# Block sums of weights and gate halves: from GpSimd additions to copies and adding transfers in DRAM

## The chip, the cores and the metric

One Trainium2 chip, of which one core is used. A core has TensorE (PE in the profile), VectorE (DVE), ScalarE (ACT), GpSimd (POOL) and SyncE (SP), and 16 DMA engines which the queues of SP, ACT and POOL share. The metric is the device time of one execution of the kernel in microseconds, lower is better.

## The reference, cut to what matters

An encoder layer in float32, sequence 1024, model width 1024, feed-forward width 2816:

```python
mod = jax.nn.silu(c) @ w_ada + b_ada
sh1, sc1, gt1, sh2, sc2, gt2 = jnp.split(mod[:, None, :], N_MOD, axis=-1)
h = rmsnorm(x, norm1_g) * (1.0 + sc1) + sh1
u, v, q, k, va, gate_a, gate_b = jnp.split(h @ w_in, cuts, axis=-1)
a_out = gmlp_branch(u, v, gm_v_g, gm_w_s, gm_b_s) @ w_a
b_out = window_attention_branch(q, k, va, q_norm_g, k_norm_g, attn_sink) @ w_b
merged = jax.nn.sigmoid(gate_a) * a_out + jax.nn.sigmoid(gate_b) * b_out
x = x + gt1 * (merged @ w_o)
h2 = rmsnorm(x, norm2_g) * (1.0 + sc2) + sh2
f_gate, f_up = jnp.split(h2 @ w_ffn_in, 2, axis=-1)
x = x + gt2 * ((jax.nn.silu(f_gate) * f_up) @ w_ffn_out)
```

## The kernel before, in words

**Products.** Each float32 product is made of three products of rounded parts: high by high, high by low, low by high. `unit` turns a loaded tile `raw` (128 x 1024, 512 KB) into `wh`, cast by ScalarE, and `wl`, what is left, subtracted by VectorE (in the attention loops by GpSimd). There are three buffers each of `raw`, `wh` and `wl`. Activations are split in the same way.

**Blocks.** The products with w_u and w_v, with the gates' weights w_ga and w_gb, with w_o and the feed-forward weights are done as two by two blocks in seven block products rather than eight. That needs sums of the weights' four blocks and sums or differences of the activations' blocks. With blocks a11, a12 (of w_u or w_ga) and a21, a22 (of w_v or w_gb), the weights' sums are a21+a22, a11+a21+a22, a11+a21 and a12+a11+a21+a22. The sums of before are additions on GpSimd between tiles in SBUF.

**Stages**, with their place in the profiled execution:
- 0 to 65 us: projection of the first half of the sequence to q and k in eight steps (`half(0)`), beside the adaLN loads; from the first step on `x_square(k)` loads rows of the second half's x into an `hs` tile (two buffers), squares them on ScalarE and adds on GpSimd (L553).
- 65 to 110: the bridge: u and v products, norms of q and k (`kd`, `q_norm`), and `u_sums` (L870), which loads blocks of w_u and w_v, makes eight sums of 128 x 1024 on GpSimd and stores them to `usd` and `utd` (L244). `bridge_copy` (L745) stores the first products to `uvd`.
- 110 to 190: the attention loop of the first half, eight steps. Gate products (`gate_filler`, L809) fill TensorE's gaps; each evicts its bank through a `t` tile (four buffers) to `gd` in DRAM by ScalarE's queue (`astore`, L139). `x_mod` loads and modulates the second half's x and stores it to `x1sd`.
- 190 to 260: projection and bridge of the second half, with `block_sums` of activations on VectorE.
- 260 to 340: its attention loop. `gate_raw_sum` (L763) loads w_gb and half of w_ga and adds them on GpSimd.
- 340 to 425: the u and v stage: `load_uv` reads `uvd`, two GpSimd additions of 128 x 2048 (L1036 and L1037) merge them, then products, GELU, norm and mixing.
- 425 to 550: the loop over eight rows d of gates and branch projections. `gate_prep` (L1107) loads w_ga[d], w_gb[d] and gd[d] and makes five sums on GpSimd; `merge` stores the merged rows to `md` (L1180).
- 550 to 650: the products with w_o: `load_wo` (L1190) loads four 1 MB blocks, `wsum` (L1274) makes four sums on GpSimd; residual, gt1 scaling (`gated`) and sums of squares (`ssq`, L1293, additions on GpSimd by default).
- 650 to the end: the feed-forward part, which the change does not touch.

**What sets the order.** Each engine runs its instructions in program order; SP's loads and, within a half's loop, everything else are kept in the order in which the code is written (`in_order`). A DMA is issued by SP (`load`, L133), ScalarE (`astore`, L139) or GpSimd (`store`, L136), in line with that engine's other instructions. The work of a half's loop is a list of jobs: per step, one `run_jobs` and the fillers.

Every engine instruction goes through one wrapper, so the profile shows L75 for all of them; they are told apart by tile names.

## Time and profile before

| What | Value |
|---|---|
| Time, median of 3 runs | 1308.88 us (1307.22 to 1310.63) |
| The profiled execution's own time | 1312.13 us |
| Its span in the profile | 1310.3 us |
| Mean granted TensorE clock | 0.979 |
| TensorE busy | 1230.9 us (94%) |
| DMA moved | 261.17 MB, 199 GB/s over the span |

The profile is of one execution; durations read from it stand against its own 1312.13 us, and 3.25 us are taken off to compare with the median. "Busy" leaves out the issuing of DMAs. A table by stretch gives the busy time of each engine between two moments of the span; "released by" (<-) names what ended the idle time ahead of an instruction.

### The profile page before, as it was taken

Reading aid. Unit: us, or ns where it says so; the run is one execution under the profiler, and the core shown is the slowest. Engines: PE = TensorE matmul, PEld = TensorE weight load, DVE = VectorE, ACT = ScalarE, POOL = GpSimd, SP = SyncE. Lnnn points to the kernel's source line nnn. Section 1 sums busy time; section 2 is a strip of 40 time slices with the busy share of each in tenths; the row PEclk is TensorE's granted clock in tenths of the full one; section 3 lists DMA queues with packets and bytes.
Section 4 is the critical chain, followed back from the end, with each engine's and each line's share of the span. In section 5 each row is a group of like instructions: output and inputs, shape, how many; then the busy total and the mean of one; then the engine's idle time right before and its main releaser. Section 6 shows DMA issues by size and latency. Waiting matters only on the chain.

```text
span 1310.3 us, 15346 instructions
## 1 busy us (share of the span) xinstructions
PE 1230.9 (94%) x5522; PEld 1003.2 (77%) x5522; DVE 961.1 (73%) x1445; ACT 568.5 (43%) x928; POOL 281.6 (21%) x229
## 2 busy tenths in 40 slices
PE   6879998999969998988999999999999999999998
PEld 4757777887758777776788888888888887888887
DVE  8999868977587776789899766766665765555646
ACT  5447762677563121225555333333333333533342
POOL 1583320433362242263010001000001000010001
PEclk9998999999989999998999999999999999999999
DMA  9855468642734656641541344555437547986652
GB/s 366 304 220 216 159 249 286 231 140 98 296 138 177 256 226 234 247 193 65 183 155 49 113 161 175 202 195 199 146 143 243 191 162 262 322 306 205 193 173 97
DMA packets 82255, 261.17 MB, mean 199 GB/s; under 512 B 8706, under 2 KB 8706, under 8 KB 72835
## 3 DMA queue, kind: packets, MB, share of 16 engines
q1 hardware_dynamic: 61490, 175.25, 37.7%
q0 software_dynamic: 12624, 70.26, 14.7%
q10 hardware_dynamic: 8064, 14.68, 3.0%
q8 instruction: 43, 0.70, 0.2%
q14 instruction: 34, 0.27, 0.1%
HBM read 188.85 MB, written 71.30 MB: 199 GB/s over the span
## 4 chain that ended last, share of the span: by engine, by line
PE 64%; DVE 16%; DMA 10%; ACT 4%; issue 4%; POOL 1%; SPq 0%; ACTq 0%; DVEq 0%; POOLq 0%
PE at L75 40%; PE mm L75 24%; DVE mid L75 7%; DMA raw<-in_w_gb_dram 3%; DVE wl L75 3%; DVE j L75 2%; DMA raw<-in_w_q_dram 1%; ACT wh L75 1%; DMA mid<-in_xT_dram 1%; DVE kd L75 1%; POOL raw L75 1%; DMA mid<-in_w_ada_dram 1%; DMA md<-j 1%; DMA mid<-x0d 1%; ACT lb L75 1%
## 5 line engine op out<-in xcount | busy, mean ns | idle before, releaser
L75 PE MATMUL mm<-mid,wh 128*128 128x512 f32 x736 | 233.1, 398 | 1.7 <-DVE mid L75 1.7
L75 PE MATMUL at<-mid,wh 128*128 128x512 f32 (+1 forms) x728 | 228.7, 396 | 6.1 <-ACT mid L75 2.9
L75 DVE TENSOR_TENSOR wl<-raw,wh 128x1024 fp32r<-128x1024 f32 x116 | 153.8, 1326 | 81.6 <-ACT wh L75 81.3
L75 ACT CAST wh<-raw 128x1024 fp32r<-128x1024 f32 x126 | 131.8, 1048 | 116.4 <-PE at L75 38.1
L75 PEld LDWEIGHTS at<-mid,wh 128*128 128x128 f32 x728 | 138.6, 192 | 38.2 <-ACT mid L75 3.3
L75 PEld LDWEIGHTS mm<-mid,wh 128*128 128x128 f32 x736 | 138.3, 190 | 31.5 <-DVE mid L75 2.3
L75 PE MATMUL at<-mid,wl 128*128 128x512 f32 (+1 forms) x364 | 144.1, 396 | 8.9 <-DVE wl L75 8.9
L75 PE MATMUL mm<-mid,wl 128*128 128x512 f32 x368 | 145.6, 396 | 4.6 <-DVE wl L75 4.6
L75 PE MATMUL at<-j,wh 128*128 128x512 f32 (+1 forms) x464 | 143.6, 391 | 0.0
L75 PE MATMUL mm<-wh,mid 128*128 128x512 f32 x320 | 110.8, 414 | 11.6 <-DVE mid L75 6.5
L75 PEld LDWEIGHTS at<-j,wh 128*128 128x128 f32 x464 | 86.5, 188 | 20.2 <-DVE mid L75 0.2
L75 DVE TENSOR_TENSOR wl<-ws,wh 128x1024 fp32r<-128x1024 f32 (+1 forms) x55 | 62.0, 1127 | 44.2 <-ACT wh L75 44.2
L75 PE MATMUL at<-j,wl 128*128 128x512 f32 (+1 forms) x232 | 90.7, 391 | 0.0
L75 PEld LDWEIGHTS at<-mid,wl 128*128 128x128 f32 x364 | 69.8, 192 | 25.5 <-DVE wl L75 11.0
L75 PEld LDWEIGHTS mm<-mid,wl 128*128 128x128 f32 x368 | 70.1, 191 | 21.1 <-DVE wl L75 5.9
L75 PEld LDWEIGHTS mm<-wh,mid 128*128 128x128 f32 x320 | 63.0, 200 | 25.7 <-ACT mid L75 13.3
L75 ACT CAST wh<-ws 128x1024 fp32r<-128x1024 f32 (+1 forms) x55 | 53.5, 974 | 57.7 <-DVE ws L75 41.2
L75 PE MATMUL mm<-wl,mid 128*128 128x512 f32 x160 | 66.4, 415 | 0.4 <-DVE wl L75 0.4
L75 PE MATMUL mm<-j,wh 128*128 128x512 f32 x176 | 57.2, 406 | 4.9 <-DVE j L75 4.9
L75 DVE TENSOR_TENSOR ol<-raw,oh 128x1024 fp32r<-128x1024 f32 x30 | 36.7, 1224 | 32.4 <-ACT oh L75 30.6
L75 ACT ACTIVATE j<-j 128x512 f32<-128x512 f32 x32 | 19.9, 631 | 92.8 <-DVE j L75 92.8
L75 DVE TENSOR_TENSOR mid<-mid,mid 128x512 fp32r<-128x512 f32 (+3 forms) x43 | 50.6, 1209 | 8.8 <-DMA mid<-x1sd 5.1
(251 smaller groups left out, 2457.2 us busy)
## 6 DMA issues: line engine op xcount, KB each, us to landing
raw<-in_w_gate_dram SPq DMA_DIRECT2D x28, 512.0 KB, 4.7
j<-in_w_ada_dram SPq DMA_DIRECT2D x13, 1024.0 KB, 5.4
tA<-hid POOLq DMA_DIRECT2D x11, 1024.0 KB, 5.0
tB<-hid POOLq DMA_DIRECT2D x11, 1024.0 KB, 4.9
wo<-in_w_out_dram POOLq DMA_DIRECT2D x22, 512.0 KB, 6.3
wS<-wo POOLq DMA_DIRECT2D x11, 1024.0 KB, 5.5
raw<-wS SPq DMA_DIRECT2D x44, 256.0 KB, 3.4
raw<-tB SPq DMA_DIRECT2D x44, 256.0 KB, 4.4
```

Source lines behind the costliest of these rows:

```text
L75: ins = f(*args, **kw)
```

## The change

Twelve DRAM tensors hold the weights' block sums: `wus` for u and v, `wgs` for the gates, `wos` for w_o, 1 to 4 each. A sum is begun by `sum_copy`, a DMA from DRAM to DRAM of one block on ScalarE's queue, and finished by `sum_add`, a DMA from DRAM to DRAM on GpSimd's queue that adds its source to what lies there. There are 16 copies and 16 adds of 1 MB (the gates' in two halves): four copies in the last steps of the first half's projection, eight copies and eight adds, one a step, in its loop, four copies and eight adds in the second half's loop. Sums 2 and 4 add another sum: 2 adds sum 1, and 4 adds sum 2. The stages behind load finished sums.

The halves of the gates are merged in the same way: the first half's loop stores each first-half gate product to three columns of `gd` and each second one to the fourth, 32 stores instead of 16; the second half's loop adds its products to `gd` by 16 adding DMAs from SBUF. So with `uvd`: four stores in the first half, now on ScalarE's queue, and two adds of 1 MB in the second. In the w_o stage w_o's blocks and sums come through `raw` tiles, seven 1 MB blocks rather than four, two evictions scale by gt1 on ScalarE, and x is added to them by two adding DMAs. The squares' additions in `x_square` and `ssq` move to VectorE; `x_square` runs at steps 6 and 7 (0 and 1, then 2, 3, 4) and in the bridge (5, 6, 7).

```diff
@@ -243,3 +243,5 @@
     gd = rows_d(KT, "gd", w=2048)
-    usd, utd = rows_d(2, "usd", w=2048), rows_d(2, "utd", w=2048)
+    wus = [None] + [rows_d(2, f"wus{i}", w=UNIT) for i in range(1, 5)]
+    wgs = [None] + [rows_d(KT, f"wgs{i}") for i in range(1, 5)]
+    wos = [None] + [rows_d(1, f"wos{i}", w=2048) for i in range(1, 5)]
     md = [rows_d(KT, f"md{h}") for h in range(2)]
@@ -539,2 +541,27 @@
 
+    def acc_dma(dst, src):
+        ins = nc.gpsimd.dma_start(dst, src, accum_op=ALU.add, max_dma_last_dim=4096)
+        if in_order[0]:
+            tc.keep_in_program_order(ins)
+
+    SUMS = {}
+
+    def sum_begin(dst, src):
+        load(dst, src)
+
+    w_gah = [w_ga[:, :, i * Q : (i + 1) * Q] for i in range(2)]
+    w_gbh = [w_gb[:, :, i * Q : (i + 1) * Q] for i in range(2)]
+    SUMS["u"] = (wus, (w_u[0:2], w_u[2:4], w_v[0:2], w_v[2:4]))
+    SUMS["g0"] = ([x and x[0:4] for x in wgs], [x[0:4] for x in w_gah + w_gbh])
+    SUMS["g1"] = ([x and x[4:8] for x in wgs], [x[4:8] for x in w_gah + w_gbh])
+    SUMS["o"] = (wos, tuple(w_o[i : i + 1] for i in range(4)))
+
+    def sum_copy(n, i):
+        s, (a11, a12, a21, a22) = SUMS[n]
+        astore(s[i], {1: a21, 2: a11, 3: a21, 4: a12}[i])
+
+    def sum_add(n, i):
+        s, (a11, a12, a21, a22) = SUMS[n]
+        acc_dma(s[i], {1: a22, 2: s[1], 3: a11, 4: s[2]}[i])
+
     next_x = {}
@@ -552,3 +579,3 @@
             A.activation(q, xk, AF.Square)
-            G.tensor_tensor(ssn, ssn, q, op=ALU.add)
+            V.tensor_tensor(ssn, ssn, q, op=ALU.add)
 
@@ -686,3 +713,6 @@
                 store(x0d[k], x[:, :HALF])
-                x_square(k)
+                if k > 3:
+                    sum_copy(*(("u", 3), ("g0", 3), ("g1", 3), ("u", 1))[k - 4])
+                for i in ((), (0, 1), (2, 3, 4))[max(k - 5, 0)]:
+                    x_square(i)
             else:
@@ -725,3 +755,3 @@
         bsrc = [w_u[k] for k in range(4)] if hf == 0 else [
-            usd[0][:, :UNIT], usd[1][:, :UNIT], w_v[2], w_v[3]]
+            wus[3][0], wus[3][1], w_v[2], w_v[3]]
         bridge = [unit(bsrc[0], V)]
@@ -748,3 +778,7 @@
                 (V.tensor_copy if t % 2 else A.copy)(u[:, t, :], vps[t])
-            store(uvd[2 * hf + i], flat(u))
+            if hf:
+                acc_dma(uvd[2 + i], flat(u))
+            else:
+                for j in ((0, 2, 3), (1,))[i]:
+                    astore(uvd[j], flat(u))
 
@@ -764,6 +798,4 @@
             r = wpool.tile([P, UNIT], F32, tag="raw", name=nm("raw"))
-            load(r, w_gb[d])
-            x = stream("hs")
-            load(x, w_ga[d][:, :Q])
-            G.tensor_tensor(r[:, :Q], r[:, :Q], x, op=ALU.add)
+            load(r[:, :Q], wgs[3][d])
+            load(r[:, Q:], w_gb[d][:, Q:])
             return r
@@ -774,3 +806,3 @@
             srcs = [lambda d=d: gate_raw_sum(d) for d in range(KT)]
-            srcs += [utd[j][:, :UNIT] for j in range(2)]
+            srcs += [wus[2][j] for j in range(2)]
         units = []
@@ -820,4 +852,10 @@
                 A.copy(c, gbanks[d])
-                i = ((2, 0), (3, 1))[hf][ks[-1] // 4]
-                astore(gd[d][:, i * Q : (i + 1) * Q], c)
+                i = ks[-1] // 4
+                if hf:
+                    acc_dma(gd[d][:, (3 - 2 * i) * Q : (4 - 2 * i) * Q], c)
+                elif i:
+                    astore(gd[d][:, :Q], c)
+                else:
+                    for j in (1, 2, 3):
+                        astore(gd[d][:, j * Q : (j + 1) * Q], c)
             if ks[-1] == KT - 1:
@@ -869,14 +907,2 @@
 
-            def u_sums(j):
-                a, b = midt(F32, 2), midt(F32, 2)
-                for i in range(2):
-                    load(a[:, i, :], w_v[2 * i + j])
-                    load(b[:, i, :], w_u[2 * i + j])
-                return [lambda: G.tensor_tensor(a[:, 1], a[:, 0], a[:, 1], op=ALU.add),
-                        lambda: G.tensor_tensor(a[:, 0], a[:, 0], b[:, 0], op=ALU.add),
-                        lambda: (G.tensor_tensor(b[:, 0], b[:, 0], a[:, 1], op=ALU.add),
-                                 store(usd[j], flat(a))),
-                        lambda: (G.tensor_tensor(b[:, 1], b[:, 1], b[:, 0], op=ALU.add),
-                                 store(utd[j], flat(b)))]
-
 
@@ -893,3 +919,4 @@
         if hf == 0:
-            us = u_sums(0)
+            for i in (5, 6, 7):
+                x_square(i)
         bridge.append(unit(bsrc[2], V))
@@ -903,4 +930,2 @@
             col_rstd(next_x["ss"], NT, rcol[1])
-            for f in us:
-                f()
         bridge_product(2)
@@ -941,5 +966,2 @@
                 prepare(V)
-            if t == 0 and hf == 0:
-                for f in u_sums(1):
-                    f()
         bridge_copy(1)
@@ -949,2 +971,4 @@
             jobs.extend(lambda k=k: x_mod(k) for k in range(KT + 1))
+            wjobs = [("u", 3), ("g0", 3), ("g1", 3), ("u", 1), ("g0", 1), ("g1", 1), ("u", 2), ("g0", 2)]
+            cjobs = [("u", 2), ("g0", 1), ("g1", 1), ("g0", 2), ("g1", 2), ("u", 4), ("g0", 4), ("g1", 4)]
         else:
@@ -966,2 +990,4 @@
 
+            wjobs = [("g1", 2), ("u", 4), ("g0", 4), ("g1", 4), ("o", 3), ("o", 1), ("o", 2), ("o", 4)]
+            cjobs = [("o", 3), ("o", 1), ("o", 2), ("o", 4)]
             jobs.extend([lambda: None] * 3)
@@ -987,2 +1013,5 @@
                 values(base + i, koff, kv, pts, vts, i, oH, oL)
+            if cjobs:
+                sum_copy(*cjobs.pop(0))
+            sum_add(*wjobs.pop(0))
             fill(FB)
@@ -1016,3 +1045,3 @@
     t1f = jt(F32, 4)
-    uv_raw = [raw_unit(usd[0][:, UNIT:])]
+    uv_raw = [raw_unit(wus[1][0])]
     load(flat(t1f), t1d[0])
@@ -1026,6 +1055,6 @@
     load_uv(0)
-    uv_raw.append(raw_unit(usd[1][:, UNIT:]))
+    uv_raw.append(raw_unit(wus[1][1]))
     vgain_b = stream("hs")
     load(vgain_b, rowv[:GW].partition_broadcast(P))
-    uv_raw.append(raw_unit(utd[0][:, UNIT:]))
+    uv_raw.append(raw_unit(wus[4][0]))
     load_uv(2)
@@ -1035,4 +1064,2 @@
     lows(T1J, t1f)
-    G.tensor_tensor(flat(c2), flat(c2), flat(up1), op=ALU.add)
-    G.tensor_tensor(flat(c1), flat(c1), flat(up1), op=ALU.add)
 
@@ -1107,13 +1134,12 @@
     def gate_prep(d):
-        ga, gb = raw_unit(w_ga[d]), raw_unit(w_gb[d])
         g = gates[d] = jt(F32, 4)
+        r = wpool.tile([P, UNIT], F32, tag="raw", name=nm("raw"))
+        load(r[:, :Q], wgs[2][d])
+        load(r[:, Q:], wgs[1][d])
+        r4 = wpool.tile([P, UNIT], F32, tag="raw", name=nm("raw"))[:, :Q]
+        load(r4, wgs[4][d])
         load(flat(g), gd[d])
-        G.tensor_tensor(gb[:, Q:], gb[:, :Q], gb[:, Q:], op=ALU.add)
-        G.tensor_tensor(gb[:, :Q], ga[:, :Q], gb[:, Q:], op=ALU.add)
-        G.tensor_tensor(ga[:, Q:], ga[:, Q:], gb[:, :Q], op=ALU.add)
-        for i in (1, 3):
-            G.tensor_tensor(g[:, i, :], g[:, i, :], g[:, 2, :], op=ALU.add)
-        u = unit(None, V, gb)
+        u = unit(None, V, r)
         h, l = tmp(F32R), tmp(F32R)
-        split(ga[:, Q:], h, l)
+        split(r4, h, l)
         gunits[d] = u, (h, l)
@@ -1143,3 +1169,3 @@
     uv_product(ws, T1J, False)
-    ws = [unit(None, V, uv_raw[2]), unit(utd[1][:, UNIT:], V)]
+    ws = [unit(None, V, uv_raw[2]), unit(wus[4][1], V)]
     v_chain(0, c2)
@@ -1187,7 +1213,5 @@
     wabs = {0: unit(w_ab[0])}
-    wq4 = {}
 
-    def load_wo(i):
-        wq4[i] = (jt if i < 2 else midt)(F32, 4)
-        load(flat(wq4[i]), w_o[i])
+    def ounits(src):
+        return [unit(src[:, j * UNIT : (j + 1) * UNIT], V) for j in range(2)]
 
@@ -1231,3 +1255,2 @@
         if d == 6:
-            load_wo(0)
             load_m(1, 0)
@@ -1235,3 +1258,2 @@
             load_m(0, 0)
-            load_wo(1)
             M11 = (jt(F32R, 4), jt(F32R, 4))
@@ -1245,8 +1267,5 @@
         if d == 6:
-            wu = [unit(None, V, flat(wq4[0])[:, j * UNIT : (j + 1) * UNIT]) for j in range(2)]
+            wu = ounits(w_o[0])
     assert not ada_queue
 
-    def ounits(i, eng=None):
-        return [unit(None, eng, flat(wq4[i])[:, j * UNIT : (j + 1) * UNIT]) for j in range(2)]
-
     def oprod(us, t, banks, first, ks=range(4)):
@@ -1273,7 +1292,2 @@
 
-    def wsum(out, a, b):
-        for j in range(2):
-            js = slice(j * UNIT, (j + 1) * UNIT)
-            G.tensor_tensor(flat(out)[:, js], flat(a)[:, js], flat(b)[:, js], op=ALU.add)
-
     def xload(q, hf):
@@ -1292,3 +1306,3 @@
 
-    def ssq(x, first, ss, eng=G):
+    def ssq(x, first, ss, eng=V):
         if first:
@@ -1306,11 +1320,6 @@
     oprod(wu, M11, sA, True)
-    for i in (2, 3):
-        load_wo(i)
     load_m(0, 1)
     block("M21", mf[1, 0])
-    wu = ounits(1)
+    wu = ounits(w_o[1])
     h2m.append(xload(0, 0))
-    wsum(wq4[0], wq4[0], wq4[2])
-    wq4[4] = jt(F32, 4)
-    wsum(wq4[4], wq4[0], wq4[3])
     m11, m12, m21, m22 = mf[0, 0], mf[0, 1], mf[1, 0], mf[1, 1]
@@ -1324,3 +1333,3 @@
     block("n2", m11)
-    wu = ounits(4)
+    wu = ounits(wos[2][0])
     ss = ss_tile()[:, :HALF]
@@ -1335,4 +1344,2 @@
     oprod(wu, blk["n2"], sA, False)
-    wsum(wq4[1], wq4[1], wq4[4])
-    wsum(wq4[2], wq4[2], wq4[3])
     block("T3", t3f)
@@ -1340,15 +1347,15 @@
                            op0=ALU.mult, op1=ALU.subtract)
-    wu = ounits(0)
-    vk = jt(F32, 4)
+    wu = ounits(wos[3][0])
+    vk = midt(F32, 4)
     for d in range(4):
-        A.copy(vk[:, d, :], sA[d])
+        A.activation(vk[:, d, :], sA[d], AF.Copy, scale=pg1(d))
     oprod(wu, blk["T3"], sA, False)
     block("T4", m21)
-    wu = ounits(3)
-    wk = jt(F32, 4)
+    wu = ounits(w_o[3])
+    wk = midt(F32, 4)
     for d in range(4):
-        A.copy(wk[:, d, :], sA[d])
+        A.activation(wk[:, d, :], sA[d], AF.Copy, scale=mg1(d))
     oprod(wu, blk["T4"], sA, False)
     block("t1", m12)
-    wu = ounits(2)
+    wu = ounits(wos[1][0])
     for d in range(4):
@@ -1358,6 +1365,6 @@
         keep_x1(1, 0, d, o)
-    x1b1 = xload(1, 1)
-    x1b0 = xload(0, 1)
-    for d in range(4):
-        gated(x1b1[:, d, :], wk[:, d, :], mg1(d))
+    for q, t in ((1, wk), (0, vk)):
+        nc.gpsimd.dma_start(t, xT[q * HALF : (q + 1) * HALF, HALF:].rearrange("(a p) t -> p a t", p=P),
+                            accum_op=ALU.add)
+    x1b1, x1b0 = wk, vk
     sB = [mm_bank() for _ in range(4)]
@@ -1369,3 +1376,3 @@
     oprod(wu, blk["t1"], sB, True, range(3, 4))
-    wu = ounits(1)
+    wu = ounits(wos[4][0])
     h2[0] = [[hid(), hid()], [hid(), hid()]]
@@ -1388,4 +1395,2 @@
         keep_x1(1, 1, d, o)
-    for d in range(4):
-        gated(x1b0[:, d, :], vk[:, d, :], pg1(d))
     raw0 = raw_unit(w_gate[0])
```

Where the instructions stand is shown at three places. POOL in the first half's bridge, from the norm of the second half's rows (rcol is the column of reciprocal roots) on; mid are u_sums' tiles, and later the splits of the attention's output. Before:

```order
L75 TENSOR_TENSOR rcol_125<-ms_759,nhalf 128x4
L75 TENSOR_TENSOR mid_721<-mid_721 128x1024
L75 TENSOR_TENSOR mid_721<-mid_721,mid_722 128x1024
L75 TENSOR_TENSOR mid_722<-mid_722,mid_721 128x1024
L136 DMA usd<-mid_721 128x2048
L75 TENSOR_TENSOR mid_722<-mid_722 128x1024
L136 DMA uvd<-mid_793 128x2048
L136 DMA utd<-mid_722 128x2048
```

And of the change, from the same instruction on:

```order
L75 TENSOR_TENSOR rcol_135<-ms_767,nhalf 128x4
L543 DMA wus_110<-in_w_u_dram 256x1024
L75 TENSOR_TENSOR mid_1024<-xs_1149,mid_1023 64x4x128
L543 DMA wgs_114<-in_w_ga_dram 512x512
L75 TENSOR_TENSOR wl_1166<-raw_1003,wh_1165 128x1024
L75 TENSOR_TENSOR mid_1024<-xs_1253,mid_1023 64x4x128
L543 DMA wgs_114<-in_w_ga_dram 512x512
```

The sums and their stores are gone from the bridge, and adding DMAs stand in the loop between the splits.

ACT in one step of the first half's loop (gd are the gate stores, t the evicted gate banks, pH the softmax's high part). Before:

```order
L139 DMA x1sd<-hs_1318 128x512
L75 COPY t_246_1330<-mm_1065 128x512
L139 DMA gd<-t_246_1330 128x512
L75 CAST wh_1346<-raw_1169 128x1024
L75 COPY xs_1359<-at_1352 64x512
L75 CAST mid_1031<-xs_1359 64x4x128
L75 COPY t_253_1370<-mm_1333 128x512
L139 DMA gd<-t_253_1370 128x512
L75 CAST pH_1400<-at_1395 128x512
```

And of the change:

```order
L139 DMA x1sd<-hs_1322 128x512
L75 COPY t_242_1334<-mm_1061 128x512
L139 DMA gd<-t_242_1334 128x512
L75 CAST wh_1350<-raw_1169 128x1024
L75 COPY xs_1363<-at_1356 64x512
L75 CAST mid_1023<-xs_1363 64x4x128
L139 DMA wgs_113<-in_w_ga_dram 512x512
L75 COPY t_249_1376<-mm_1337 128x512
L139 DMA gd<-t_249_1376 128x512 x3
L75 CAST pH_1408<-at_1403 128x512
```

A copy from DRAM to DRAM stands ahead of the second gate eviction, and that eviction is stored three times.

ACT at the end of the first half's projection (t are squares of the second half's rows hs, wh the high part of the bridge's first weights). Before:

```order
L75 ACTIVATE t_69_543<-hs_541 128x512
L75 ACTIVATE mid_225<-mid_131,mod 128x512
L75 ACTIVATE mid_132<-mid_131,mod 128x128
L75 CAST wh_620<-raw_618 128x1024
L75 ACTIVATE mid_131<-mid_131,mod 128x128
L75 ACTIVATE t_71_583<-hs_581 128x512
L75 COPY mid_624<-mm_228 128x512
```

And of the change:

```order
L75 ACTIVATE mid_141<-mid_141,mod 128x128
L139 DMA wus_108<-in_w_v_dram 16x16384
L75 ACTIVATE t_61_572<-hs_570 128x512
L75 ACTIVATE t_63_577<-hs_575 128x512
L75 ACTIVATE t_65_582<-hs_580 128x512
L75 CAST wh_619<-raw_617 128x1024
L75 COPY mid_623<-mm_238 128x512
```

Three squares stand together ahead of the cast, behind the issue of a copy.

## The prediction

> **What bounds the kernel now.** The profile's first page comes first: engines, and the chain that ended last by engine.
>
> ```profile
> PE 1230.9 (94%) x5522; PEld 1003.2 (77%) x5522; DVE 961.1 (73%) x1445; ACT 568.5 (43%) x928; POOL 281.6 (21%) x229
> PE 64%; DVE 16%; DMA 10%; ACT 4%; issue 4%; POOL 1%; SPq 0%; ACTq 0%; DVEq 0%; POOLq 0%
> ```
>
> TensorE (PE) is the bound, and its gaps are what can be won: 1310.3 − 1230.9 = 79 us of span, and the clock it loses after gaps. GpSimd (POOL) is 21% busy and 1% of the chain, so its own time is worth little; what counts is what it does to VectorE (DVE). The table by stage comes next. Columns: stretch, length, busy time (and count) of PE, weight loads, DVE, ACT, POOL, then granted clock, DMA share, GB/s. The feed-forward part from 650 on is left alone by the change.
>
> ```profile
> 45.00:110.00 65.00, 50.20 (x254) 41.55 (x253) 61.19 (x96) 29.98 (x64) 45.35 (x30) 0.89 0.68 252
> 110.00:190.00 80.00, 75.34 (x376) 60.79 (x375) 65.19 (x168) 61.26 (x144) 22.39 (x14) 0.99 0.52 181
> 190.00:260.00 70.00, 65.34 (x331) 54.82 (x330) 56.80 (x96) 33.06 (x63) 18.00 (x15) 0.96 0.75 268
> 260.00:340.00 80.00, 77.56 (x388) 63.86 (x389) 55.53 (x151) 60.54 (x138) 27.72 (x18) 1.00 0.43 152
> 340.00:425.00 85.00, 72.63 (x333) 59.09 (x332) 65.45 (x83) 41.77 (x70) 38.20 (x21) 0.92 0.51 191
> 425.00:550.00 125.00, 115.47 (x479) 92.36 (x478) 89.89 (x140) 27.34 (x38) 39.10 (x25) 0.96 0.65 243
> 550.00:650.00 100.00, 90.84 (x383) 72.57 (x382) 89.77 (x87) 41.91 (x61) 32.88 (x12) 0.95 0.40 150
> ```
>
> PE loses 14.8 us in the first row, 12.4 at 340–425, 9.5 at 425–550 and 9.2 at 550–650: these are the stages with GpSimd sums. The two attention loops (110–190 and 260–340) lose 4.7 and 2.4, and DMA is idle half of each. The change takes sums out of the four, and puts transfers into the two.
>
> **What the sums cost.** First the chain in the first bridge, then DVE and POOL in the u/v stage and DVE in the w_o stage by the timeline (start, length, and in brackets the wait ahead).
>
> ```profile
> 77.34 0.63 DVE kd L75 x3
> ...
> 81.78 4.79 DVE kd L75 x3
> ...
> 86.59 5.39 DVE kd L75 x3
> ```
>
> ```profile
> 344.54 4.60 POOL L75 TENSOR_TENSOR mid<-mid,mid 128x2048 f32<-128x2048 f32 x1 [8.11 <-DMA mid<-uvd]
> ```
>
> ```profile
> 349.17 2.48 DVE L75 TENSOR_TENSOR mid<-mm,mid 128x512 f32<-128x512 f32 x4 [5.10 <-POOL mid L75]
> 351.57 1.21 DVE L75 TENSOR_TENSOR wl<-raw,wh 128x1024 fp32r<-128x1024 f32 x1
> 353.30 5.05 DVE L75 TENSOR_TENSOR wl<-raw,wh 128x1024 fp32r<-128x1024 f32 x1 [0.51 <-ACT wh L75]
> ```
>
> ```profile
> 574.62 11.30 DVE L75 TENSOR_TENSOR mid<-mid,mid 128x512 fp32r<-128x512 f32 x4
> ...
> 600.36 2.48 DVE L75 TENSOR_TENSOR mid<-mid,mid 128x512 fp32r<-128x512 f32 x4
> ```
>
> One DVE instruction with two inputs in SBUF takes several times longer while GpSimd adds: 0.63 becomes 4.79 and 5.39, 1.21 becomes 5.05, 2.48 becomes 11.30. So a sum on GpSimd stalls the engine that feeds PE.
>
> *First bridge, 45–110.* The two stretched kd pieces are worth 4.79 + 5.39 − 2 × 0.63 = 8.9 us on the chain, and the clock of 0.89 over 50.2 us busy another 5.5, of which I take 3.6. Against it stand two things. Moving the squares' adds puts seven on DVE, 0.68 each by this group of the same shape, 4.8 us; but DVE's weight splits in the projection, 2.30 beside GpSimd's adds instead of 1.21, give 4 × 1.1 = 4.4 back.
>
> ```profile
> L75 DVE TENSOR_TENSOR ss<-ss,t 128x512 f32<-128x512 f32 x8 | 5.4, 679 | 0.1
> ```
>
> ```profile
> L75 DVE TENSOR_TENSOR wl<-raw,wh 128x1024 fp32r<-128x1024 f32 x4 | 9.2, 2301 | 0.0
> ```
>
> And the squares now come three at a time, with two buffers for the loaded rows, so the third load starts only after the first square, and ACT waits for it in order, ahead of the bridge's first weight cast. One such landing is the 4.2 us of hs below; I charge it once. Net 12.5 − 4.2 − 0.4 = **8**.
>
> *u/v stage, 340–425.* The wait of 5.10 and the stretch of 3.8: **9**. The adding transfers that replace these sums are done before the stage.
>
> *Gate loop, 425–550.* PE's waits here and GpSimd's sums per step:
>
> ```profile
> PE at L75 <- DVE wl L75: 8.9, 5, 2.8
> PE mm L75 <- DVE wl L75: 0.7, 2, 0.3
> ```
>
> ```profile
> L75 POOL TENSOR_TENSOR j<-j 128x512 f32<-128x512 f32 x16 | 31.3, 1977 | 0.0
> L75 POOL TENSOR_TENSOR raw<-raw,raw 128x512 f32<-128x512 f32 x16 | 21.9, 1370 | 1.3
> ```
>
> The chain of five sums (about 3 × 1.37 + 2 × 1.98 = 8.1 us a step) ahead of the weight split goes. The 9.6 us of waits go, and the clock (0.96 of 115 us, 4.6) returns a little: **10**. The loads shrink from 2.0 to 1.75 MB a step, so they stay covered.
>
> *w_o stage, 550–650.* The waits:
>
> ```profile
> PE mm L75 <- DVE wl L75: 3.9, 1, 3.9
> PE at L75 <- ACT mid L75: 2.9, 1, 2.9
> ```
>
> These 6.8 and the clock's 4.5 go; six adds of squares move to DVE (6 × 0.68 = 4.1). Seven 1 MB weights are loaded instead of four, 3 × 2.6 us of transfer (price below) under 60 us of free DMA time. The eight scalings by gt1 become ACT's, in evictions it did already, and two adding transfers bring x in, under some products. **7**.
>
> Gains: 8 + 9 + 10 + 7 = **34 us**. The most that can come back is 8.9 + 5.5 in the bridge, the 12.4 us that PE idles at 340–425, and idle time with clock loss in the other two, 9.5 + 4.6 and 9.2 + 4.5: 55; nothing comes back if DVE's own rows bind there.
>
> **What the transfers cost.** No row of before shows a copy from DRAM to DRAM, or an adding transfer. The nearest rows are a stretch of pure loads and one of loads beside stores, both with DMA full, and the issues of the tiles concerned:
>
> ```profile
> 10.00:15.00 5.00, 1.49 (x7) 1.49 (x8) 4.14 (x5) 3.36 (x4) 0.00 (x0) 1.00 1.03 426
> 195.00:200.00 5.00, 5.00 (x25) 4.16 (x25) 3.68 (x3) 3.00 (x5) 0.00 (x0) 1.00 1.05 411
> ```
>
> ```profile
> gd<-t ACTq DMA_DIRECT2D x32, 256.0 KB, 4.5
> hs<-in_xT_dram SPq DMA_DIRECT2D x16, 256.0 KB, 4.2
> ```
>
> At 411 GB/s a pass of 1 MB (1.049 million bytes) is 2.6 us of all DMA engines, one of 256 KB 0.65. A copy is one pass if the engines read and write at once as they do for a load, two if each side is paid; an add, with two reads and a write, lies between one pass and three. I take **one for a copy** (nearest row: 411 with loads and stores mixed) and **two for an add** (the middle).
>
> *First loop, 110–190*: it uses 0.52 × 80 = 41.6 us. New on ACT's queue: 16 more gate stores (each first half is written three times), 10.4, and 8 copies, 20.8: the loop's own transfers come to 72.8 of 80. The 8 adds on GpSimd's queue take 41.6 more: 114 in all, 34 over. Most of these adds are wanted only from 230 on, so they may fall back behind the loop's; whether they do depends on how the engines share between the queues, which no row shows. I charge half: **17**.
>
> *Second loop, 260–340*: 34.4 in use, 3.9 less for gate loads, 4 copies 10.4, 8 adds 41.6, and 16 gate halves that are added rather than stored, 10.4 more: 93, 13 over, half of it **6**. The first adds behind them are wanted at 340.
>
> The waits come with it. A transfer issued on SP or ACT waits, in the program's list of waits, for the one eight before it on these two queues together. With six a step on ACT and two or three on SP, that is about the step before, 10 us ago; gate evictions, the cast pH of the next softmax and the weight casts are queued behind an ACT issue that waits. On GpSimd, an add waits for its copy or, as (o,2) does, for the add a step earlier; behind it stand the splits wl and mid<-xs, and behind those PE's gate fillers. At 5.2 us a transfer both fit into a step.
>
> Sum: 1312.1 − 34 + 17 + 6 = 1301 for the profiled execution. That execution is 3.3 us above the median of the runs, so **1298** for the runs.
>
> **A rule weighed.** No run shows the price of a copy in DRAM. The Trainium skill, "DMA: Bandwidth & Descriptors", section "Latency and other measured facts", gives copies between HBM tensors 207 to 214 GB/s per direction; read as the rate of a copy that is an estimate of 5 us for 1 MB, two passes instead of my one. By it the sum is the slower rival's, 1333.
>
> **Rivals.** *Hidden altogether.* An add costs one pass, or the adds yield to the loop's own transfers. For it: the first loop's 72.8 us without its adds fit into 80, and so do 34.4 − 3.9 + 12 × 2.6 = 61.7 in the second at one pass each. Against: 72.8 of 80 leaves little for waits. Then nothing is paid: 1312 − 34 = 1278, **1275** for the runs; with all 55 us of gain 1254.
>
> *Slower: the loops become bound by DMA.* Copies and adds cost two passes each, and the queues share evenly. The first loop's transfers come to 41.6 + 10.4 + 41.6 + 41.6 = 135, 55 over; the second's to 103, 23 over. Half the free DMA time of the stages behind (17.5 at 190–260, and up to the overshoot at 340–425) drains 9 and 11, and 58 us remain: 1312 − 34 + 58 = 1336, **1333** for the runs. It decides from the point where the overshoot passes the 34 us of gain. For it: the first bridge already ends with DMA 0.68 busy, and GpSimd already waits for a gate store, and ACT for a sum's round trip through DRAM, as these rows show; against it: no row of the table has DMA over 0.75 for a whole stage.
>
> ```profile
> POOL mid L75 <- DMA gd<-t: 8.4, 1, 8.4
> ...
> ACT wh L75 <- DMA raw<-usd: 12.6, 2, 8.0
> ```
>
> *An add at half a copy's rate.* With copies at two passes and adds at four, the first loop has 177 us of transfers and the second 166: 97 − 9 and 86 − 20 after draining, 154 over, **1429** for the runs. For it speaks only that an add must read twice; the trace has none. The Trainium skill, "Collectives: The Full Stack", section "The bandwidth ceiling: the fold count and why AG ≠ RS ≠ AR", says that an adding transfer needs two source reads on one ring and so runs at half a copy's rate. No run here shows it.
>
> **How the numbers follow.** The forecast has 0.37; hidden 0.24; slower, bound by DMA, 0.28; half rate 0.06; the rest, 0.05, are gains eaten by DVE, near 1312. A change under 0.3%, about 4 us, can't be told from none in a measurement of this kernel. The forecast's own range is 1283 to 1312: with a third of the 23 us charged 1283, with the whole overshoot of 47 less some 10 drained and the same gain 1312. Cases of both signs hold much of the chance, so the range goes from 1262 (hidden, with 13 of the 21 us of further gain) to 1345 (bound by DMA, with 12 us less gain), leaving out the half-rate case and the tails, about 0.18. Faster: 0.24 hidden, 0.31 of the forecast: 0.55. Same: 0.04 of the forecast and 0.05: 0.09. Slower: 0.36.
>
> **What would show it.** Right: kd x3 back at 0.6 us, the four mid<-mid,mid of the w_o stage at 2.5, DVE's wait for POOL at 344 gone, PE's waits for wl near zero in the gate loop, and DMA at 0.9 or more in both loops with the loops a little over 80 us. Wrong on transfers: loops of 80 us with DMA at 0.8 (hidden), or of 100 and more, with ACT waiting for gd, wgs or wus, and POOL for its adds (bound by DMA). Wrong on gains: PE still waiting for DVE in the four stages, with DVE at its short times, or ACT held at the bridge by hs for longer than 4 us.

## The result, and the profile after

The changed kernel takes **1358.59 us** (median of 4 runs, 1357.18 to 1359.49) against 1308.43 us before (median of 4): a ratio of 1.038, 95% interval 1.0362 to 1.0398. The forecast was 1298, with a range of 1262 to 1345. The profiled execution of the changed kernel took 1358.86 us, its span is 1357.1 us and its mean granted clock 0.958.

First the page of the changed kernel: engines, and the chain that ended last.

```profile
PE 1230.4 (91%) x5522; PEld 1007.1 (74%) x5522; DVE 902.0 (66%) x1450; ACT 570.2 (42%) x928; POOL 157.4 (12%) x178
PE 70%; DMA 15%; DVE 7%; ACT 3%; issue 3%; ACTq 1%; SPq 0%; POOL 0%; DVEq 0%; POOLq 0%
```

GpSimd has 124 us less work, VectorE 59 less, and DVE's share of the chain fell from 16% to 7%; DMA's rose from 10% to 15%. What was to be removed is removed, and TensorE's gaps grew all the same, from 79 to 127 us.

**Where the time went.** TensorE runs the same 5522 matmuls in nearly the same order (by tile and shape 114 places differ, in short runs), so the two traces can be laid beside each other by their count: for each moment of before, the moment at which the other trace has counted as many. In brackets, how much longer (+) or shorter the stretch is that ends there.

| Stretch of before ends at | what it is | changed kernel |
|---|---|---|
| 45 | projection, first part | 41.9 (−3.1) |
| 70 | projection, end | 76.5 (+9.6) |
| 120 | bridge | 119.0 (−7.5) |
| 190 | first attention loop | 230.9 (+41.8) |
| 260 | second projection and bridge | 316.8 (+16.0) |
| 340 | second attention loop | 410.8 (+14.0) |
| 425 | u/v stage | 497.6 (+1.8) |
| 550 | gate loop | 606.2 (−16.4) |
| 650 | w_o stage | 691.5 (−14.7) |
| 720 | start of the feed-forward part | 767.1 (+5.5) |
| 1300 | feed-forward part | 1346.9 (−0.2) |

The stages that lost their GpSimd sums gained 31 us in gate loop and w_o stage alone; 72 us are lost from the first loop to the second. (The expectations below split the same 72 us at somewhat earlier marks, as 32, 26 and 13.) The table by stretch shows it, in the changed kernel's own times (columns as in the prediction):

```profile
118.00:220.00 102.00, 63.76 (x272) 51.10 (x271) 53.38 (x133) 48.22 (x115) 23.58 (x17) 0.81 0.95 266
220.00:316.00 96.00, 77.23 (x378) 63.52 (x376) 60.51 (x106) 39.36 (x74) 19.07 (x14) 0.90 0.73 234
316.00:409.00 93.00, 80.35 (x387) 66.44 (x386) 58.38 (x149) 57.83 (x135) 43.32 (x36) 0.91 0.98 225
...
490.00:603.50 113.50, 113.50 (x500) 93.57 (x499) 80.25 (x138) 29.15 (x41) 0.00 (x0) 1.00 0.66 243
603.50:690.00 86.50, 85.97 (x385) 70.76 (x385) 69.15 (x89) 41.66 (x59) 4.59 (x3) 1.00 0.70 222
```

The gate loop is now TensorE without a gap at full clock (113.50 of 113.50). The two attention loops have DMA 0.95 and 0.98 busy, where before had 0.52 and 0.43, and TensorE is idle for 38 of 102 us in the first, with the clock down to 0.81. (The first row stops 11 us short of that loop's end at 230.9.)

The chain in order of time (start, length, what), at its long pieces and at one issue:

```profile
53.32 7.23 DMA hs<-in_xT_dram
...
63.91 5.66 DMA raw<-in_w_u_dram
...
132.58 10.16 DMA raw<-in_w_ga_dram
...
146.53 20.92 DMA wgs<-in_w_ga_dram
167.45 0.02 issue
167.47 0.50 ACTq L139
167.97 0.04 issue
168.01 1.56 ACT pH L75 x3
...
184.48 12.68 DMA raw<-in_w_q_dram
197.18 0.03 SPq L133
197.20 0.04 issue
197.24 17.06 DMA mid<-x0d
...
229.19 15.70 DMA mid<-x1sd
```

A weight copy lands after 20.92 us; ScalarE's queue had been held by it, and the softmax's cast pH stands behind the issue that it released. Then a weight load, the load of x0d and that of x1sd follow one another. Before, the loads of x0d and x1sd took 9.9 and 6.1 us. The issues with their median time to landing say the same; gd by ScalarE took 4.5 us before, where its 32 stores stood in both loops and not all in the first.

```profile
gd<-t ACTq DMA_DIRECT2D x32, 256.0 KB, 9.4
...
wgs<-in_w_ga_dram ACTq DMA_DIRECT2D x4, 1024.0 KB, 15.6
wgs<-wgs POOLq DMA_DIRECT2D x4, 1024.0 KB, 25.6
...
gd<-t POOLq DMA_DIRECT2D x16, 256.0 KB, 19.8
mid<-uvd SPq DMA_DIRECT2D x4, 1024.0 KB, 19.8
```

### The profile page after: what moved, and what is told of

The parts are those of the page before. It is cut to its first block, busy times and chain, and to the rows that moved or that the text cites. A ratio compares the mean times of both kernels' runs of the same rounds, so it can differ in the third digit from the quotient of the medians.

```text
span 1357.1 us, 15317 instructions
## 1 busy us (share of the span) xinstructions
PE 1230.4 (91%) x5522; PEld 1007.1 (74%) x5522; DVE 902.0 (66%) x1450; ACT 570.2 (42%) x928; POOL 157.4 (12%) x178
## 4 chain that ended last, share of the span: by engine, by line
PE 70%; DMA 15%; DVE 7%; ACT 3%; issue 3%; ACTq 1%; SPq 0%; POOL 0%; DVEq 0%; POOLq 0%
PE at L75 42%; PE mm L75 28%; DVE mid L75 3%; DMA gd<-t 2%; DMA mid<-uvd 2%; DMA wgs<-in_w_ga_dram 2%; DVE wl L75 1%; DMA mid<-x0d 1%; DMA mid<-x1sd 1%; ACT mid L75 1%; DMA raw<-in_w_q_dram 1%; DMA raw<-in_w_gb_dram 1%; DMA mid<-in_w_ada_dram 1%; DMA raw<-in_w_ada_dram 1%; ACT wh L75 1%
## 5 line engine op out<-in xcount | busy, mean ns | idle before, releaser
L75 PE MATMUL mm<-mid,wh 128*128 128x512 f32 x736 | 236.3, 402 | 0.0
L75 PE MATMUL at<-mid,wh 128*128 128x512 f32 (+1 forms) x728 | 224.0, 389 | 2.0 <-ACT wh L75 2.0
L75 ACT CAST wh<-raw 128x1024 fp32r<-128x1024 f32 x140 | 146.6, 1050 | 172.1 <-PE at L75 44.9
L75 DVE TENSOR_TENSOR wl<-raw,wh 128x1024 fp32r<-128x1024 f32 x130 | 159.8, 1232 | 84.8 <-ACT wh L75 83.9
L75 PEld LDWEIGHTS mm<-mid,wh 128*128 128x128 f32 x736 | 141.2, 195 | 30.3 <-DVE mid L75 0.4
L75 PEld LDWEIGHTS at<-mid,wl 128*128 128x128 f32 x364 | 68.8, 189 | 14.2
L75 DVE TENSOR_TENSOR xs<-at,xs 128x512 f32<-128x512 f32 (+1 forms) x45 | 31.0, 689 | 55.7 <-ACT xs L75 29.7
L75 DVE TENSOR_TENSOR mid<-mid,mid 128x512 fp32r<-128x512 f32 (+3 forms) x43 | 39.4, 945 | 40.1 <-DMA mid<-x0d 19.1
```

What stands on the lines that cost most here:

```text
L75: ins = f(*args, **kw)
```

## The experiments

Theory A: the DMA engines are full in the two attention loops, and what does not fit is paid there. Rival B: ScalarE's and GpSimd's in-order waits cost, whatever the load.

**1. No adds.** The two loops issue their copies, and no `sum_add`; the sums lack their second addend.

```diff
-            sum_add(*wjobs.pop(0))
```

> The 16 adding transfers between DRAM tensors are left out, so the blocks' sums lack their second addend; the 16 copies, the tripled gate stores and the adds of gates and u stay. Theory A (the DMA engines are full in the two attention loops, and the adds are what fills them): at two passes of 2.6 us each, 83 us of transfers go, and with them the 32 + 26 + 13 us that the first loop, the projection behind it and the second loop lost against before: 1280 to 1295 us. Rival B (ScalarE's queue waits behind its own copies and stores; the adds matter little): 1330 or more, with the first loop still about 100 us long.

Measured: 1314.18 us (ratio to before 1.003, 1.0016 to 1.0043). Neither: 44 us less than the changed kernel, and yet the stretch up to 190 is 43.0 us longer than before, as long as with the adds; the projection behind it (+1.3), the second loop (−3.8) and the u/v stage (−12.5) are cured.

**2. Adds as plain copies.** Same queue, places and bytes.

```diff
-        acc_dma(s[i], {1: a22, 2: s[1], 3: a11, 4: s[2]}[i])
+        ins = nc.gpsimd.dma_start(s[i], {1: a22, 2: s[1], 3: a11, 4: s[2]}[i], max_dma_last_dim=4096)
+        if in_order[0]:
+            tc.keep_in_program_order(ins)
```

> The 16 adding transfers become plain copies of the same bytes on the same queue at the same places, so that the sums are overwritten by one addend. Tells what adding costs over copying. If an add takes two passes and a copy one, 16 x 2.6 = 42 us of transfers go and 25 to 45 us of the time: 1315 to 1335 us. If an add takes what a copy takes: 1355 to 1362 us.

Measured: 1330.76 us, 28 us less, as expected for an add of two passes. The shares of GpSimd's queue (packets, MB, share of 16 engines' span) give the prices: of the changed kernel, of run 1 and of run 2.

```profile
q0 software_dynamic: 20752, 87.04, 23.1%
```

```profile
q0 software_dynamic: 15376, 70.26, 17.2%
```

```profile
q0 software_dynamic: 19728, 87.04, 20.6%
```

0.231 x 1357.1 = 313.5 us with the adds, 0.172 x 1310.4 = 225.4 without: 88 us for 16, **5.5 us an add** of 1 MB. 0.206 x 1328.2 = 273.6 with copies in their place: 48 us, **3.0 us a copy**. Both near the prices of the forecast, 5.2 and 2.6.

**3. Three gate stores in one.** The same bytes by 16 fewer issues.

```diff
-                    for j in (1, 2, 3):
-                        astore(gd[d][:, j * Q : (j + 1) * Q], c)
+                    astore(gd[d][:, Q:].rearrange("p (j q) -> p j q", j=3),
+                           c.unsqueeze(1).to_broadcast([P, 3, Q]))
```

> The three stores of each first-half gate product become one transfer that writes all three columns: the same bytes, 16 fewer issues on ScalarE's queue. Theory A (bytes): 1352 to 1364 us. Rival B (the number of transfers, each waiting for the one eight before it): the first loop gets at least 10 us shorter, 1330 to 1348 us.

Measured: 1355.14 us, in theory A's range: bytes and not issues. Rival B gets little (the first loop is 6 us shorter).

**4. Squares one a step.**

```diff
-                for i in ((), (0, 1), (2, 3, 4))[max(k - 5, 0)]:
-                    x_square(i)
+                x_square(k)
```

with the three of the bridge taken out.

> The squares of the second half's rows go back to one per step of the projection, as in the kernel before, with their additions left on VectorE. If the stop of TensorE at 60 to 72 us comes from ScalarE waiting for the loads of those rows, it goes: 1347 to 1353 us. If it comes from the copies that fill the DMA engines just there, it stays: 1356 to 1362 us.

Measured: 1352.34 us. Projection's end and bridge go from +9.6 and −7.5 to +5.1 and −13.5, and the first part, where squares now stand again, gives 2 of these 10 us back. So the bunched loads of hs cost 8 us, not the 4.2 that I charged: the load of w_u stood behind them on SP, at 63.91 us in the chain above and at 51.8 in this run.

**What run 1 pointed to.** With no add, what fills the stretch up to 190? VectorE's timeline at the end of the first loop, before:

```profile
176.39 1.41 DVE L75 TENSOR_SCALAR lb<-lb,den 128x384 f32<-128x384 f32 x4
180.96 2.29 DVE L75 TENSOR_TENSOR mid<-mid,mid 128x2048 f32<-128x2048 f32 x1 [3.15 <-DMA mid<-x0d]
```

and of the changed kernel:

```profile
214.39 2.29 DVE L75 TENSOR_TENSOR mid<-mid,mid 128x2048 f32<-128x2048 f32 x1 [19.13 <-DMA mid<-x0d]
216.60 1.88 DVE L75 TENSOR_TENSOR pL<-at,pH 128x512 fp32r<-128x512 f32 x3
218.40 0.15 DVE L75 TENSOR_TENSOR es<-rows,nmx 128x4 f32<-128x4 f32 x1
218.47 0.74 DVE L75 SCALAR_TENSOR_TENSOR hs<-hs,mod,ss 128x512 f32<-128x512 f32 x1
219.13 0.74 DVE L75 SCALAR_TENSOR_TENSOR mid<-hs,mod,mid 128x512 fp32r<-128x512 f32 x1
219.79 0.15 DVE L75 TENSOR_TENSOR den<-den,es 128x4 f32<-128x4 f32 x1
219.98 0.18 DVE L75 RECIPROCAL den<-den 128x4 f32<-128x4 f32 x1
220.19 1.41 DVE L75 TENSOR_SCALAR lb<-lb,den 128x384 f32<-128x384 f32 x4
```

The first block sum of the second projection (the difference in `block_sums`, k = 4), which needs x0d from DRAM, stands behind the last step's scaling of lb before, and ahead of that step's pL, es, hs and lb after (pL, es, den and lb belong to the softmax, hs are rows of x). It is not held in program order, so the build may move it, and the diff doesn't show that it did. VectorE waits 19.13 us for x0d with the last step of attention behind it; that step's hs is what is stored to x1sd, and the load of x1sd follows. Two trips to DRAM that overlapped now follow one another. This is theory C.

In run 1 the build moved more. Its chain has the first difference behind x0d, and then three others and the store of one, t1d, behind the load of x1sd and ahead of the next softmax:

```profile
179.69 12.29 DMA mid<-x0d
...
206.51 7.86 DMA mid<-x1sd
...
214.49 2.30 DVE mid L75
...
216.82 4.50 DVE mid L75 x2
...
221.61 4.18 DMA t1d<-mid
```

**5. The order mended, all transfers kept.**

```diff
+                in_order[0] = True
                 block_sums(k, hH, hL)
+                in_order[0] = False
```

> The changed kernel with all its transfers; only the block sums of activations of the second half's projection are held in program order, so that on VectorE the 128x2048 difference of x0d stands behind the last attention step, as in the kernel before, and not ahead of it. Theory C (a good part of the loss is this order: VectorE waits for the x0d load with the last step, the x1sd store and the x1sd load behind it): 20 to 30 us go, 1328 to 1340 us. Theory A (the transfers alone): the same transfers wait elsewhere, 1350 to 1362 us.

Measured: 1340.49 us, 18 less than the changed kernel: half a microsecond above C's range, and nearly 10 below A's. Up to 260 this kernel needs 297.3 us instead of 316.8. The three lines hold every block sum of that projection, and with them about 20 instructions on VectorE, four on ScalarE and 28 places on TensorE change order; the 18 us are those of the order, and that the one difference makes them all is not shown. The first loop is still 36.8 us longer than before, the second 14.0, and the chain of this kernel shows the transfers again:

```profile
136.24 25.22 DMA wgs<-in_w_gb_dram
...
180.03 12.14 DMA wus<-in_w_u_dram
...
210.41 16.97 DMA mid<-x1sd
```

In that loop TensorE waits 19.8 us for ScalarE's pH and 12.0 for xs. ScalarE, ahead of pH, waits 14.6 us for a store to x1sd and 12.8 for a gate copy to land. No wait of GpSimd there ends with a transfer.

**6. The order mended, no adds** (as in run 1, the second addends are lacking).

> The same order, and the 16 adding transfers between DRAM tensors left out as in the first run (the sums lack their second addend). That run lost 43 us in the first loop with no add in it. Theory C: with the order mended these go for the most part, 1275 to 1288 us, and then what the adds cost is the distance to the run above, 45 us or more. Theory A: 1305 to 1316 us as without the order.

Measured: 1281.75 us, 0.978 of before (0.970 to 0.986). C again: the order alone is worth 32 us against run 1 (where four differences stood early, not one), and against run 5 the 16 adds cost 59 us. ScalarE has all the copies and stores of run 5, and still the first loop is only 8.9 us longer than before instead of 36.8, so ScalarE's waits don't cost that whatever the load, and GpSimd's, as run 5 shows, end with no transfer there: rival B doesn't explain this loop. The first loop is +8.9, the second −3.8, u/v stage −14.6, gate loop −16.4, w_o −15.1.

**7. The control:** the same three lines of run 5 in the kernel before.

> The kernel before with its block sums of activations held in program order: the control. Its difference of x0d stands behind the last step's scaling already. Both theories: within 0.5% of the kernel before, 1303 to 1315 us.

Measured: 1309.93 us, ratio 0.9986 (0.9964 to 1.0008). The order is worth nothing where it already stood right.

**8. The same transfers, spread** (with the order mended).

```diff
-            wjobs = [("u", 3), ("g0", 3), ("g1", 3), ("u", 1), ("g0", 1), ("g1", 1), ("u", 2), ("g0", 2)]
-            cjobs = [("u", 2), ("g0", 1), ("g1", 1), ("g0", 2), ("g1", 2), ("u", 4), ("g0", 4), ("g1", 4)]
+            wjobs = [("u", 3), None, ("g0", 3), None, ("g1", 3), None, None, None]
+            cjobs = [("g1", 3)] + [None] * 7
...
+            wjobs = [None, ("u", 1), None, ("u", 2), None, ("u", 4), ("g0", 1), ("g0", 2)]
+            cjobs = [("u", 1), ("u", 2), ("u", 4), None, ("g0", 1), ("g0", 2), ("g0", 4), None]
```

The rest of the gates' sums is issued in the u/v stage and those of w_o in the gate loop.

> The order mended, and the same 16 copies and 16 adds spread: three sums in the first loop instead of eight adds and eight copies, six in the second, the gates' other sums at its end, in the u/v stage and at the start of the gate loop, those of w_o in the gate loop. Theory A (DMA full in the two loops): each stage then keeps under its capacity, and the gains of 34 us remain: 1268 to 1290 us. If the total of the transfers costs, wherever it stands: 1315 to 1335 us.

Measured: 1370.74 us, slower than all. The first loop, with three adds and one copy instead of eight of each, is cured for the most part: +6.5 and +1.5 behind it, instead of +36.8 and +1.5 in run 5. But the second loop is 8 us longer, the u/v stage 26.0 and the gate loop 25.0. One wait in the gate loop shows sums that come too late for the stage that loads them:

```profile
ACT wh L75 <- DMA raw<-wgs: 17.5, 1, 17.5
```

So theory A holds for the loop that was relieved, and its expectation of the whole failed: room in the DMA engines isn't enough, a chain of copy, add, add and load must also end before its user. How much of the 51 us each of these waits makes is not known.

**9. Fewer transfers.** The order mended, squares one a step, the gates' sums 1, 2 and 4 made on GpSimd in the gate loop as before; the gates' halves are still merged by adding transfers.

```diff
-            wjobs = [("u", 3), ("g0", 3), ("g1", 3), ("u", 1), ("g0", 1), ("g1", 1), ("u", 2), ("g0", 2)]
-            cjobs = [("u", 2), ("g0", 1), ("g1", 1), ("g0", 2), ("g1", 2), ("u", 4), ("g0", 4), ("g1", 4)]
+            wjobs = [("u", 3), ("g0", 3), ("g1", 3), ("u", 1), ("u", 2), None, None, None]
+            cjobs = [("u", 2), None, ("u", 4)] + [None] * 5
...
+            wjobs = [("u", 4), None, ("o", 3), ("o", 1), ("o", 2), ("o", 4), None, None]
+            cjobs = [("o", 3), ("o", 1), ("o", 2), ("o", 4)] + [None] * 4
```

> The changed kernel with the order of the block sums mended, the squares one per step, and the gates' sums 1, 2 and 4 made on GpSimd in the gate loop again: 6 copies and 6 adds of 1 MB fewer, the rest so placed that the first loop has two copies and five adds, the second four copies and five adds; the gates' halves are still merged by adding transfers. Theory A (capacity of the loops): by passes of 2.6 us the first loop has 83 us of transfers in 80 and the second 77, so it loses under 12 us there; u/v stage -13, w_o stage -15, bridge -9, gate loop -8 for half of its sums: 1272 to 1290 us. If the number of waits or the adds themselves cost, whatever the load: the two loops still lose 25 us or more, 1300 to 1320 us.

Measured: 1292.95 us, 0.984 of before (0.980 to 0.989): 3 us above A's range and 7 below the other. First loop +8.6, second +10.2, gate loop −12.5. The two loops lose 19 us where A had under 12, the second although its 77 us of passes fit into 80, and the u/v stage gains 5 us of the 13: the count of passes is not the whole price.

**10. The w_o part alone,** on the kernel before.

> The kernel before with the w_o part of the change alone: four copies and four adds of w_o's blocks in the second loop, where before left 46 us of DMA time free (they need 31), and the w_o stage of the changed kernel. Theory A: the second loop keeps its length and the w_o stage gains its 15 us, less the 5 that the stretch behind it lost: 1294 to 1302 us. If adds cost the loop time even where there is room: 1306 to 1318 us.

Measured: 1308.24 us, ratio 0.9967 (0.9949 to 0.9985). The time is 6 us above A's range and inside that of adds which cost the loop even where there is room. The w_o stage gains 14.2 and the stretch behind it loses 6.3, as expected; but the loop, the u/v stage and the gate loop lose 2.4, 3.1 and 1.1, and 2 us are left of it in the profile. So the loop kept nearly its length, as A had it; why the two stages behind it lose is not shown.

**11. Gate halves by plain stores, merged on VectorE;** else as run 9.

```diff
+                i = ((2, 0), (3, 1))[hf][ks[-1] // 4]
+                astore(gd[d][:, i * Q : (i + 1) * Q], c)
...
+        for i in (1, 3):
+            V.tensor_tensor(g[:, i, :], g[:, i, :], g[:, 2, :], op=ALU.add)
```

> As the first kernel of this call, but the gates' products go to DRAM by 16 + 16 plain stores as in the kernel before, and the halves are merged on VectorE in the gate loop: 21 us of transfers fewer in the first loop and the second 10 to 21 fewer; 16 additions of 0.68 us more on VectorE, which is 71% busy there. Theory A: the loops lose nothing any more, the gate loop gains 3 us less: 1268 to 1284 us, at or below the first kernel of this call. If VectorE is the bound of the gate loop: 5 to 15 us above it.

(The first kernel that this expectation speaks of is run 9's.) Measured: 1280.8 us, 0.976 of before (0.972 to 0.980): in A's range, and faster than both kernels. First loop −0.6, second +3.5, gate loop −7.5 (5 us less gain than in run 9: 16 additions of 0.68 us are 11). The first loop, the second and the gate loop of this kernel by stretch:

```profile
106.60:176.00 69.40, 63.83 (x318) 51.45 (x318) 54.94 (x141) 54.07 (x123) 25.43 (x17) 1.00 0.92 257
...
246.20:329.60 83.40, 78.81 (x388) 64.44 (x387) 60.27 (x150) 60.02 (x135) 28.00 (x19) 0.98 0.93 257
...
406.70:524.20 117.50, 111.78 (x479) 88.82 (x478) 85.94 (x145) 26.40 (x37) 21.38 (x15) 1.00 0.69 253
```

DMA is 0.92 busy in the first loop, and the loop is no longer than before. In run 6 the same loop is 0.92 busy as well and 8.9 us longer, so the share alone doesn't tell where the loss begins.

**12. The w_o stage's sums of squares back on GpSimd,** else as run 11.

```diff
-    def ssq(x, first, ss, eng=V):
+    def ssq(x, first, ss, eng=G):
```

> The fastest kernel so far, with the sums of squares of the w_o stage back on GpSimd. In all kernels with the change's w_o stage the stretch behind it, 650 to 720 of the kernel before, is 5 to 7 us longer. If that is the six additions that went to VectorE (4.1 us), it goes: 1274 to 1279 us. If GpSimd's additions stall VectorE here as they do elsewhere, it is no shorter: 1280 to 1287 us.

Measured: 1278.8 us (1275.66 to 1283.09), 0.975 of before; run 11 had 1277.67 to 1284.11, so the two can't be told apart. The time lies in the range for the additions, but the stretch that it was about, behind the w_o stage, stays 5.6 us longer than before: the six additions on VectorE are not what it loses, and its cause stays open.

## Why the prediction was wrong, point by point

**Gains.** GpSimd's additions did stall VectorE, and in the gate loop and the w_o stage what was read from that came back, or more. Two groups before, and the same two after:

```profile
L75 DVE TENSOR_TENSOR mid<-mid,mid 128x512 fp32r<-128x512 f32 x32 | 30.3, 991 | 0.5 <-ACT mid L75 0.4
...
L75 DVE SCALAR_TENSOR_TENSOR kd<-kraw,krs,gqk 128x64 f32<-128x64 f32 x16 | 10.8, 714 | 0.0
```

```profile
L75 DVE TENSOR_TENSOR mid<-mid,mid 128x512 fp32r<-128x512 f32 x32 | 20.6, 683 | 5.0 <-ACT mid L75 4.9
...
L75 DVE SCALAR_TENSOR_TENSOR kd<-kraw,krs,gqk 128x64 f32<-128x64 f32 x16 | 3.8, 277 | 0.0
```

kd went from a mean of 714 ns to 277, mid from 991 to 683. Of the terms, the gate loop's 10 measured 16.4; the w_o stage's 7 measured 14.7 less 5.5 behind it, 9; the bridge's 8 measured 1, and 9 once the squares were one a step (run 4): the term for the hs loads was too small. The u/v stage's 9 became a loss of 1.8, and is a gain of 12.5 to 14.6 where the adds are left out (runs 1 and 6): its loads of uvd took 19.8 us to land instead of 9.6, beside the last adds of the second loop.

**Prices.** One pass for a copy, two for an add: right (3.0 and 5.5 us against 2.6 and 5.2). The third rival's adds of four passes didn't come. The Trainium skill, "Collectives: The Full Stack", section "The bandwidth ceiling: the fold count and why AG ≠ RS ≠ AR", has the add of a ring collective at half a copy's rate; here it is 3.0 / 5.5 = 0.55 of it, close to the rule, but from a copy at one pass, not two. The prediction's estimate of 5 us for a copy, from the Trainium skill, "DMA: Bandwidth & Descriptors", section "Latency and other measured facts", is not borne out by these 3.0 us.

**The step that failed** is "I charge half". The forecast had 34 us over in the first loop and 13 in the second, and let half of it fall back behind the loop at no cost. With the order mended, the first loop and the projection behind it lost 36.8 + 1.5 us, the second loop 14.0 (run 5): 52 us, the whole overshoot and a little more, was paid. The load does it: with three adds and one copy in the first loop (run 8) the same 38 us shrink to 8, and without adds (run 6) the loop is 8.9 us over. In the first loop nothing fell back: in run 5 its eight adds have all landed at 220.4 us, ahead of the loop's end at 226.6, and its 107.7 us at a DMA share of 1.05 hold 113 us of transfers, where the forecast's sum was 114. The loop's own transfers got slower beside the adds: in the changed kernel gd's stores by ScalarE took 9.4 us instead of 4.5, hs's loads 6.6 instead of 4.2. In run 5 ScalarE's work then stood behind these landings, and TensorE's behind ScalarE's.

**What the forecast didn't see** is the order: I showed the moves on POOL and ACT, and not those of the block sums on VectorE at the end of the loop. They cost 18 us with all transfers (run 5 against the changed kernel), and 32 without the adds (run 6 against run 1, where more of them had moved). No rival of mine held it.

Put together afterwards, from the profiled execution: 1312 − 34 + 47 (whole overshoot) + 19.5 (order, at the 260 mark) + 11 (the u/v stage, +1.8 for −9) = 1355.5, and 1358.9 was measured; the other terms' errors (bridge +7, gate loop −6.4, w_o stage −2) nearly cancel. The slower rival, with 1333, had the mechanism (bound by DMA, with the waits for wgs and gd that it named); but its copies were priced at two passes and took one, and its 20 us did not drain for nothing. That its 58 us of loss in the loops come near the 52 that were paid is luck: the two errors largely cancel.

## What to carry to other kernels

Count the passes that moved work lays on the DMA engines in the very stretch where it stands, and charge all of what is over its capacity: here all of it was paid. Leave a margin too, since the same loop at 0.92 busy lost nothing in one run and 8.9 us in another. When a change leaves instructions free to move, look for the consumer of a DRAM load that now stands ahead of the last work of the stage before. Undo the parts one by one: here a mix (u's, w_o's and one of four gate sums by transfers, the gates' other sums on GpSimd, their halves merged on VectorE) beats the kernel before by 2.4% and the changed one by more.

## What the runs showed of the hardware

A copy of 1 MB from DRAM to DRAM took 3.0 us of all DMA engines and an adding transfer 5.5, against 2.6 for a load at the 411 GB/s of the prediction's rows. In the full loops their median time to landing was up to 15.6 and 25.6 us. Taking GpSimd's sums out of the gate loop was worth 16.4 us to TensorE though GpSimd was on 1% of the chain; 12.5 of them came when only the two merges of a step went and the three sums of weights stayed (run 9).
